# FFN up-projections of a two-layer hybrid decoder: one 512-column product for the rounded input and its residual

## The chip, the cores and the metric

The kernel runs on one core of one Trainium2 chip. The metric is the time of one execution on the device in microseconds (us). Three runs of the kernel before the change gave 2309.21, 2311.9 and 2316.67 us; the median is 2311.9.

PE below is TensorE (matrix products), DVE is VectorE, ACT is ScalarE, POOL is GpSimd, SP is SyncE, which issues the DMA transfers.

## The reference

Two decoder layers over a sequence of 256 tokens, width 2048. Each has a token mixer (layer 0: forgetting attention, layer 1: sliding-window attention with sinks) and then a gated feed-forward network (FFN) with a causal depthwise convolution of width 3. All is float32. The change touches the FFN:

```python
def conv_ffn(h, w_up, conv_w, conv_b, w_down):        # w_up (2048, 2*5632), w_down (5632, 2048)
    S = h.shape[1]
    u = h @ w_up
    up = jnp.pad(u, ((0, 0), (CONV_WIDTH - 1, 0), (0, 0)))
    u = sum(up[:, j:j + S] * conv_w[j] for j in range(CONV_WIDTH)) + conv_b
    g, val = u[..., :D_FF], u[..., D_FF:]
    return (jax.nn.silu(g) * val) @ w_down

for i in range(DEPTH):                                # DEPTH = 2
    mod = c_act @ ada_w[i] + ada_b[i]
    sh1, sc1, g1, sh2, sc2, g2 = jnp.split(mod[:, None, :], 6, axis=-1)
    h = x * (1.0 + sc1) + sh1
    y = fox_attention(h, ...) if i % N_MIXERS == 0 else swa_attention(h, ...)
    x = layer_norm(DEEPNORM_ALPHA * x + (1.0 + g1) * y, ln_mix_g[i], ln_mix_b[i])
    h = x * (1.0 + sc2) + sh2
    y = conv_ffn(h, ffn_w_up[i], ffn_conv_w[i], ffn_conv_b[i], ffn_w_down[i])
    x = layer_norm(DEEPNORM_ALPHA * x + (1.0 + g2) * y, ln_ffn_g[i], ln_ffn_b[i])
```

## The kernel before, in words

**Three products for one.** A float32 matrix is split into a rounded part (type fp32r, which PE takes in one pass) and the residual of the rounding, also fp32r. A product is then the sum of three: rounded × rounded, rounded × residual, residual × rounded. The FFN's input `h` lies transposed (features on the partitions) in `hH` (rounded) and `hL` (residual), two tiles of 16 chunks of 128 features by 256 tokens.

**The weight stream** (`stream`, L246 on). A weight tile is two chunks of 128 input features by 512 columns, 512 KB. For each tile SP issues one transfer into `w` (L256, ten buffers), ACT rounds it into `wh` (L259, four buffers), DVE subtracts to get the residual `wl` (L270, four buffers), and PE multiplies. The code lets casts and residuals of up to two tiles be written down ahead of the products of a tile (`ahead`, `settle`, `rest`).

**An up-projection** (`w_stationary`, `w_mm`) holds the weights in the array: `wh` or `wl` (128 × 128) is loaded and `hH` or `hL` (256 columns, the tokens) streams through. A block is 512 columns of the weights, that is four groups of 128 features, and takes eight tiles. Its four sums of 256 columns lie in two PSUM banks `ws`, two to a bank; a bank holds 512 float32 columns and there are eight. A tile has 2 chunks × 4 groups × 3 = 24 products. A layer has 22 such blocks, 11 for the gate and 11 for the value, in turn; both layers have 352 tiles.

**A down-projection** (`x_stationary`, `x_mm`) holds the activations and streams 512 columns of weights; a tile has 12 products, into banks `xs`.

**Evacuation** (`conv`, `evac`, `silu`, `gated` in `conv_ffn`). When a block is done, a generator is put in a list; each later tile steps every generator there once (`run_post`, called in `go`). For each group of 128 features, ACT computes the convolution's tap for the current token and the bias from PSUM into `u` (L987), and DVE adds the two earlier taps, reading PSUM again (L988, L990). One group is done every second tile. Gate blocks then take the SiLU (ACT, L1006, into `sil`); value blocks multiply by it (DVE, L1011) and split the result into the rounded and residual `gT` (L85 on ACT, L86 on DVE).

**Beside the FFN** the modulation vectors of later stages are computed: `ada_vector` streams `ada_w` (buffers `wa`, from the same pool as `w`) and DVE multiplies and adds (L385). In up-projections this goes at 0.52 steps per tile in layer 0 and 0.4 in layer 1, as long as there is work. A finished vector is summed over the partitions by PE into a bank `sm`; for a gate that is four products, each read by ACT (L397). In the first blocks of an FFN, DVE also does the layer norm's affine step on `x` (L604, L605), and PE transposes `x` into banks `sm` for `hH` and `hL`, two chunks at a time (L463).

**What sets the order.** The program is written with a tile framework: a scheduler puts each engine's instructions in a fixed order by priority and assigns buffers as they come free. On the chip each engine takes its list in that order and waits on semaphores.

Of the kernel before, what the change touches and what calls it, by code (L numbers as in the profile page):

```python
# [17 lines left out]
P = 128  # L18
# [23 lines left out]
def hybrid_trunk(ctx: ExitStack, tc: tile.TileContext, a: dict, out: bass.AP):  # L42
# [26 lines left out]
    def w_banks():  # L69
        return [bank("ws").rearrange("p (a s) -> p a s", a=2) for _ in range(2)]  # L70
# [180 lines left out]
    def stream(wsrc, row0, col, ks, use):  # L251

        for kc in ks[::2]:
            r0 = (row0 + kc) * P
            w = wtile()
            pin(nc.sync.dma_start(w, wsrc[r0:r0 + 2 * P, col:col + WB].rearrange("(k p) f -> p k f", p=P)), False)  # L256
            h = hl.tile([P, 2, WB], F32R, tag="wh", name="wh")
            l = hl.tile([P, 2, WB], F32R, tag="wl", name="wl")
            pin(nc.scalar.copy(h, w), False)  # L259

            def go(kc=kc, h=h, l=l):
                ahead[0] -= 1
                run_post()
                use(kc, h, l)
                if feeds:
                    feeds.pop(0)()
                tick()

            def residual_(w=w, h=h, l=l, go=go):
                pin(nc.vector.tensor_tensor(l, w, f32(h), op=ALU.subtract), False)  # L270
                del residuals[go]

            ahead[0] += 1
            weights.add(go)
            residuals[go] = residual_
            work.append(go)
            settle(2)
# [41 lines left out]

    def w_stationary(wsrc, col):  # L320

        ps = w_banks()
        stream(wsrc, 0, col, list(range(KC)), lambda kc, h, l: w_mm(ps, kc, h, l))
        return ps


# [122 lines left out]
            ada_step()  # L449


    hH = cst.tile([P, KC, S], F32R, name="hH")
    hL = cst.tile([P, KC, S], F32R, name="hL")
    cst.tile([P, 24], F32, name="gap")

    def mod_turn(k, n=1):
# [523 lines left out]
    def conv_ffn(l):  # L980
        w_up, w_dn = a["ffn_w_up"][l], a["ffn_w_down"][l]
        NB = DFF // WB
        cw = lambda j, f: ccol[:, l, j, f:f + 1]

        def conv(pf, f):
            u = tp.tile([P, S], F32, tag="u", bufs=3, name="u")
            nc.scalar.activation(u, pf, AF.Identity, bias=cw(CW, f), scale=cw(2, f))  # L987
            nc.vector.scalar_tensor_tensor(u[:, 1:], pf[:, :S - 1], cw(1, f), u[:, 1:],  # L988
                                           op0=ALU.mult, op1=ALU.add)
            nc.vector.scalar_tensor_tensor(u[:, 2:], pf[:, :S - 2], cw(0, f), u[:, 2:],  # L990
                                           op0=ALU.mult, op1=ALU.add)
            return u

        def evac(ps, f0, then):
            u = None
            for f in range(5):
                v = conv(ps[f // 2][:, f % 2, :], f0 + f) if f < 4 else None
                if u is not None:
                    then(f - 1, u)
                u = v  # L1000
                yield
                yield

        def silu(sil):
            def f_(f, u):
                nc.scalar.activation(sil[f // 2][:, (f % 2) * S:(f % 2 + 1) * S], u, AF.Silu)  # L1006
            return f_

        def gated(sil, gT):
            def f_(f, u):  # L1010
                nc.vector.tensor_tensor(u, u, sil[f // 2][:, (f % 2) * S:(f % 2 + 1) * S], op=ALU.mult)  # L1011
                g = gtile("gT")
                split(g[:, 0, :], g[:, 1, :], u)
                gT.append(g)
            return f_

        sbs = [(0, 6), (6, NB)]
        for si, (b0, b1) in enumerate(sbs):
            gT = []
            then(lambda: ada.update(rate=(0.52, 0.4)[l]))  # L1020
            for b in range(b0, b1):
                ps = w_stationary(w_up, b * WB)
                sil = [ttile("sil") for _ in range(2)]
                then(lambda ps=ps, b=b, sil=sil: defer(evac(ps, b * 4, silu(sil))))
                ps = w_stationary(w_up, DFF + b * WB)
                then(lambda ps=ps, b=b, sil=sil, gT=gT: defer(evac(ps, DFF // P + b * 4, gated(sil, gT))))

            def stat(kc, t, gT=gT):
                while kc >= len(gT):
                    run_post()  # L1030
                return gT[kc][:, 0, t * P:(t + 1) * P], gT[kc][:, 1, t * P:(t + 1) * P]

            def ready(si=si):
                if si == 0:
                    drain()
                ada_need(l, 5)
                ada["rate"] = (0.6, 0.4)[l]

            then(ready)
            for d in range(D // WB):  # L1040
                ps = x_stationary(w_dn, d * WB, b0 * 4, (b1 - b0) * 4, stat, (2, 4)[l] if si > 0 and d == D // WB - 1 else 0)
                then(lambda ps=ps, d=d, si=si: defer(residual(ps, d, gates[l, 5], si == len(sbs) - 1)))
        then(lambda: (flush(), ada.update(gate_free=True)))
# [54 lines left out]
```

## Time and profile before

| | |
|---|---|
| median of the runs | 2311.9 us |
| span of the profiled execution, from the first to the last instruction | 2317.4 us |
| instructions | 38661 |
| mean granted TensorE clock | 0.981 |
| DMA | 598.86 MB, 258 GB/s on average |
| layer 0: first up-projections, down-projection, second up-projections, down-projection | from 508, 786, 922 and 1152 us |
| layer 1: the same four | from 1558, 1837, 1968 and 2194 us |

The page gives no time of the profiled execution apart from its span. Up-projections run in two parts per layer, 6 gate and 6 value blocks and then 5 and 5, each followed by its share of the down-projection. In the views below, "busy" is the time in which an engine had an instruction running, "idle before" the time in which it waited ahead of a group of instructions, with what ended the wait. In rows of a chain or of a timeline, the first column is the start, the second the length, both in us.

### The profile page before, as it was taken

The page shows a single profiled execution, that of the slowest core. Times are in us where ns is not written, and L with a number is a line of the kernel's source. Part 1 is how long each engine was busy: PE and PEld are TensorE (multiplying, and loading weights), DVE is VectorE, ACT ScalarE, POOL GpSimd, SP SyncE. Part 2 cuts the span into 40 slices and gives each one's busy share as a digit, 9 for nine tenths or more (in the row PEclk, how much of TensorE's full clock was granted, in tenths as well). Part 3 has the DMA queues.
Part 4 walks back from the last instruction along what each step waited for, and adds up shares of the span by engine and source line. Part 5 has one row for each costly group of instructions (what it writes and reads, how often), then busy time and mean ns, then how long its engine had stood idle before and what let it go on. Part 6 is the DMA issues. An engine that isn't in the chain of part 4 may idle for free.

```text
span 2317.4 us, 38661 instructions
## 1 busy us (share of the span) xinstructions
PE 2243.1 (97%) x15061; PEld 2060.3 (89%) x15061; DVE 1804.0 (78%) x2609; ACT 1135.8 (49%) x1685; POOL 40.7 (2%) x79
## 2 busy tenths in 40 slices
PE   6899999999999999999999999999999999999997
PEld 5899998789999988999987778779999988999986
DVE  7788978879977876887887998899878655666655
ACT  1335654445555433454543478745555533454532
POOL 1001000010000000000001000000000000000000
PEclk9899999999999999999999999999999999999999
DMA  9998989968887897887897685778888566666663
GB/s 331 308 338 274 349 326 345 326 220 303 300 266 236 286 313 261 288 285 238 292 303 255 211 303 190 232 282 280 262 262 255 178 192 195 186 189 185 187 192 111
DMA packets 285561, 598.86 MB, mean 258 GB/s; under 512 B 20790, under 2 KB 53816, under 8 KB 285376
## 3 DMA queue, kind: packets, MB, share of 16 engines
q1 hardware_dynamic: 284768, 595.85, 78.1%
q8 instruction: 118, 1.93, 0.3%
q0 software_dynamic: 608, 0.53, 0.1%
q14 instruction: 67, 0.55, 0.1%
HBM read 594.21 MB, written 2.10 MB: 257 GB/s over the span
## 4 chain that ended last, share of the span: by engine, by line
PE 84%; DVE 10%; ACT 3%; issue 2%; DMA 1%; POOL 0%; SPq 0%; DVEq 0%; POOLq 0%; ACTq 0%
PE ws L76 49%; PE xs L76 30%; DVE wl L270 2%; DVE acc L385 2%; PE sm L76 1%; ACT wh L259 1%; PE cps L76 1%; PE o L76 1%; DVE oacc L518 1%; PE S L76 1%; PE sm L463 1%; ACT pr L645 0%; ACT pr L637 0%; PE T L657 0%; DVE x L563 0%
## 5 line engine op out<-in xcount | busy, mean ns | idle before, releaser
L270 DVE TENSOR_TENSOR wl<-w,wh 128x1024 fp32r<-128x1024 f32 x728 | 888.0, 1221 | 407.0 <-ACT wh L259 386.3
L259 ACT CAST wh<-w 128x1024 fp32r<-128x1024 f32 x728 | 762.9, 1051 | 864.6 <-PE ws L76 323.2
L76 PE MATMUL ws<-hH,wh 128*128 128x256 f32 x3328 | 945.8, 285 | 6.0 <-ACT wh L259 6.0
L76 PE MATMUL ws<-hH,wl 128*128 128x256 f32 x3328 | 936.9, 282 | 4.3 <-DVE wl L270 4.2
L76 PE MATMUL ws<-hL,wh 128*128 128x256 f32 x3328 | 939.5, 283 | 0.2 <-DVE hL L86 0.2
L76 PEld LDWEIGHTS ws<-hH,wh 128*128 128x128 f32 x3328 | 634.4, 191 | 10.0 <-ACT wh L259 6.8
L76 PEld LDWEIGHTS ws<-hH,wl 128*128 128x128 f32 x3328 | 637.2, 192 | 5.7 <-DVE wl L270 5.7
L76 PEld LDWEIGHTS ws<-hL,wh 128*128 128x128 f32 x3328 | 633.5, 190 | 2.7 <-issue 1.9
L76 PE MATMUL xs<-wh,gT 128*128 128x512 f32 x1408 | 437.2, 391 | 0.0
L385 DVE SCALAR_TENSOR_TENSOR acc<-wa,cact,acc 128x1024 f32<-128x1024 f32 x308 | 391.3, 1276 | 0.0
L76 PEld LDWEIGHTS xs<-wh,gT 128*128 128x128 f32 x1408 | 265.8, 189 | 55.4
L76 PE MATMUL xs<-wl,gT 128*128 128x512 f32 x704 | 275.1, 391 | 0.0
L76 PEld LDWEIGHTS xs<-wl,gT 128*128 128x128 f32 x704 | 133.0, 189 | 27.4
L76 PE MATMUL xs<-wl,hH 128*128 128x512 f32 x352 | 141.7, 403 | 5.5 <-DVE wl L270 5.5
L76 PE MATMUL xs<-wh,hL 128*128 128x512 f32 x352 | 140.8, 402 | 0.4 <-DVE hL L86 0.4
L76 PE MATMUL xs<-wh,hH 128*128 128x512 f32 x352 | 140.2, 408 | 0.2 <-ACT hH L473 0.2
L76 PE MATMUL xs<-wh,oT 128*128 128x512 f32 x384 | 125.4, 397 | 0.9 <-ACT pT L659 0.8
L987 ACT ACTIVATE u<-ws,ccol 128x256 f32<-128x256 f32 x176 | 96.5, 561 | 59.3 <-PE ws L76 52.0
L988 DVE SCALAR_TENSOR_TENSOR u<-ws,ccol,u 128x255 f32<-128x255 f32 x176 | 82.2, 476 | 20.5 <-ACT u L987 20.5
L76 PEld LDWEIGHTS xs<-wl,hH 128*128 128x128 f32 x352 | 67.8, 193 | 22.0 <-DVE wl L270 9.0
L76 PEld LDWEIGHTS xs<-wh,oT 128*128 128x128 f32 x384 | 72.8, 190 | 16.0 <-ACT pT L659 1.2
L990 DVE SCALAR_TENSOR_TENSOR u<-ws,ccol,u 128x254 f32<-128x254 f32 x176 | 83.1, 476 | 2.0
(211 smaller groups left out, 1564.4 us busy)
## 6 DMA issues: line engine op xcount, KB each, us to landing
w<-in_ffn_w_up_dram SPq DMA_DIRECT2D x352, 512.0 KB, 4.6
wa<-in_ada_w_dram SPq DMA_DIRECT2D x320, 512.0 KB, 5.1
w<-in_ffn_w_down_dram SPq DMA_DIRECT2D x176, 512.0 KB, 4.9
w<-in_fox_w_in_dram SPq DMA_DIRECT2D x96, 512.0 KB, 5.8
wo<-in_ada_w_dram SPq DMA_DIRECT2D x64, 512.0 KB, 6.5
w<-in_swa_w_in_dram SPq DMA_DIRECT2D x40, 512.0 KB, 4.9
w<-in_fox_w_o_dram SPq DMA_DIRECT2D x32, 512.0 KB, 6.3
w<-in_swa_w_o_dram SPq DMA_DIRECT2D x32, 512.0 KB, 5.5
```

What stands on the lines that cost most here:

```text
L76: return nc.tensor.matmul(o, lhsT, rhs, start=start, stop=stop, **kw)
L259: pin(nc.scalar.copy(h, w), False)
L270: pin(nc.vector.tensor_tensor(l, w, f32(h), op=ALU.subtract), False)
L385: pin(nc.vector.scalar_tensor_tensor(ac, wo, cact[:, k:k + 1], ac, op0=ALU.mult, op1=ALU.add), True)
L463: nc.tensor.transpose(o[:, t * P:(t + 1) * P], x[:, t, (k + j) * P:(k + j + 1) * P], ident)
L518: nc.vector.scalar_tensor_tensor(acc[:, v, k % 2, :], w[:, k, :], cact[:, kc:kc + 1], acc[:, v, k % 2, :], op0=ALU.mult, op1=ALU.add)
L987: nc.scalar.activation(u, pf, AF.Identity, bias=cw(CW, f), scale=cw(2, f))
L988: nc.vector.scalar_tensor_tensor(u[:, 1:], pf[:, :S - 1], cw(1, f), u[:, 1:], op0=ALU.mult, op1=ALU.add)
L990: nc.vector.scalar_tensor_tensor(u[:, 2:], pf[:, :S - 2], cw(0, f), u[:, 2:], op0=ALU.mult, op1=ALU.add)
```

## The change

`hH` and `hL` become the two halves of one tile `hHL`, so that for each chunk the rounded and the residual tokens lie side by side, 512 columns. One product of `wh` with these 512 columns takes the place of two of 256. Its sum is 512 columns wide and fills a bank: the left half collects rounded × rounded (and the residual weights' products), the right half rounded weights × residual tokens. A block thus takes four banks, named `wd`, instead of two. In a tile, the eight wide products come first, the eight with `wl` last. At the evacuation ACT copies the right half into a new tile `s`, and DVE adds the left half to it (`summed`); the convolution reads `s`. The generator's steps are placed anew: a group every tile, six steps in place of ten. The scratch for POOL's DMA descriptors goes to 1024. The first layer's attention keeps `w_banks` and `w_mm`.

```diff
--- before.py
+++ after.py
@@ -319,8 +319,17 @@
 
     def w_stationary(wsrc, col):
 
-        ps = w_banks()
-        stream(wsrc, 0, col, list(range(KC)), lambda kc, h, l: w_mm(ps, kc, h, l))
+        ps = [bank("wd") for _ in range(4)]
+
+        def use(kc, h, l):
+            cells = [(i, f) for i in range(2) for f in range(4)]
+            for i, f in cells:
+                mm(ps[f], h[:, i, f * P:(f + 1) * P], hHL[:, kc + i].rearrange("p a s -> p (a s)"),
+                   start=kc + i == 0)
+            for i, f in cells:
+                mm(ps[f][:, :S], l[:, i, f * P:(f + 1) * P], hH[:, kc + i, :], stop=kc + i == KC - 1)
+
+        stream(wsrc, 0, col, list(range(KC)), use)
         return ps
 
 
@@ -449,8 +458,8 @@
             ada_step()
 
 
-    hH = cst.tile([P, KC, S], F32R, name="hH")
-    hL = cst.tile([P, KC, S], F32R, name="hL")
+    hHL = cst.tile([P, KC, 2, S], F32R, name="hHL")
+    hH, hL = hHL[:, :, 0, :], hHL[:, :, 1, :]
     cst.tile([P, 24], F32, name="gap")
 
     def mod_turn(k, n=1):
@@ -982,23 +991,28 @@
         NB = DFF // WB
         cw = lambda j, f: ccol[:, l, j, f:f + 1]
 
-        def conv(pf, f):
+        def summed(pf):
+            s = tp.tile([P, S], F32, tag="s", bufs=3, name="s")
+            nc.scalar.copy(s, pf[:, S:])
+            nc.vector.tensor_tensor(s, pf[:, :S], s, op=ALU.add)
+            return s
+
+        def conv(s, f):
             u = tp.tile([P, S], F32, tag="u", bufs=3, name="u")
-            nc.scalar.activation(u, pf, AF.Identity, bias=cw(CW, f), scale=cw(2, f))
-            nc.vector.scalar_tensor_tensor(u[:, 1:], pf[:, :S - 1], cw(1, f), u[:, 1:],
+            nc.scalar.activation(u, s, AF.Identity, bias=cw(CW, f), scale=cw(2, f))
+            nc.vector.scalar_tensor_tensor(u[:, 1:], s[:, :S - 1], cw(1, f), u[:, 1:],
                                            op0=ALU.mult, op1=ALU.add)
-            nc.vector.scalar_tensor_tensor(u[:, 2:], pf[:, :S - 2], cw(0, f), u[:, 2:],
+            nc.vector.scalar_tensor_tensor(u[:, 2:], s[:, :S - 2], cw(0, f), u[:, 2:],
                                            op0=ALU.mult, op1=ALU.add)
             return u
 
         def evac(ps, f0, then):
-            u = None
-            for f in range(5):
-                v = conv(ps[f // 2][:, f % 2, :], f0 + f) if f < 4 else None
+            s = u = None
+            for f in range(6):
                 if u is not None:
-                    then(f - 1, u)
-                u = v
-                yield
+                    then(f - 2, u)
+                u = conv(s, f0 + f - 1) if s is not None else None
+                s = summed(ps[f]) if f < 4 else None
                 yield
 
         def silu(sil):
@@ -1083,7 +1097,7 @@
     from concourse import mybir as _mybir
     from concourse.bass_utils import run_bass_kernel_spmd as _run
 
-    nc = _bacc.Bacc("TRN2", target_bir_lowering=False, num_devices=1)
+    nc = _bacc.Bacc("TRN2", target_bir_lowering=False, num_devices=1, dynamic_dma_scratch_size=1024)
     arrays, args = {}, {}
     for name in _INS:
         v = _np.ascontiguousarray(inputs[name])
```

The scheduler's lists show what moved. The numbers behind names tell buffers apart; "waits" names the semaphores of an engine. First, PE's list at the start of the fourth block of layer 0's second part, before:

```order
L76 MATMUL ws_10300<-hH_125,wh_10304 128x256 [waits Activation_49]
L76 MATMUL ws_10300<-hL_126,wh_10304 128x256
L76 MATMUL ws_10300<-hH_125,wl_10305 128x256 [waits DVE_49]
L76 MATMUL ws_10300<-hH_125,wh_10304 128x256
L76 MATMUL ws_10300<-hL_126,wh_10304 128x256
L76 MATMUL ws_10300<-hH_125,wl_10305 128x256
L76 MATMUL ws_10301<-hH_125,wh_10304 128x256
```

and with the change:

```order
L76 MATMUL wd_9565<-hHL_125,wh_9571 128x512 [waits Activation_49]
L76 MATMUL wd_9566<-hHL_125,wh_9571 128x512 [waits PE_49]
L76 MATMUL wd_9567<-hHL_125,wh_9571 128x512 [waits PE_49]
L76 MATMUL wd_9568<-hHL_125,wh_9571 128x512 [waits PE_49]
L76 MATMUL wd_9565<-hHL_125,wh_9571 128x512
L76 MATMUL wd_9566<-hHL_125,wh_9571 128x512
L76 MATMUL wd_9567<-hHL_125,wh_9571 128x512
L76 MATMUL wd_9568<-hHL_125,wh_9571 128x512
L76 MATMUL wd_9565<-hHL_125,wl_9572 128x256 [waits DVE_49]
L76 MATMUL wd_9566<-hHL_125,wl_9572 128x256
```

The three narrow products of a group become a wide one at the head of the tile and a narrow one at its end; the first use of `wl` moves from the third product to the ninth.

Second, DVE's list in layer 0's first part, before the first residual (`wl_5652`) of the third block; `x` is the affine step, `acc` the modulation vector:

```order
L988 SCALAR_TENSOR_TENSOR u_5581<-ws_4977,ccol_120,u_5581 128x255
L270 TENSOR_TENSOR wl_5615<-w_5612,wh_5614 128x1024 [waits DMAHW5_49,PE_49,Activation_49]
L990 SCALAR_TENSOR_TENSOR u_5581<-ws_4977,ccol_120,u_5581 128x254 [waits DVE_49]
L604 SCALAR_TENSOR_TENSOR x_108<-x_108,ln_5354 128x512
L385 SCALAR_TENSOR_TENSOR acc_5129<-wa_5642,cact_111,acc_5129 128x1024 [waits DMAHW6_49]
L605 SCALAR_TENSOR_TENSOR x_108<-ln_5356,x_108 128x512 [waits DVE_49]
L604 SCALAR_TENSOR_TENSOR x_108<-x_108,ln_5354 128x512
L270 TENSOR_TENSOR wl_5652<-w_5649,wh_5651 128x1024 [waits DMAHW7_49,PE_49,Activation_49]
```

and with the change, where that residual is `wl_5563`, five rows further on:

```order
L1003 SCALAR_TENSOR_TENSOR u_5471<-s_5440,ccol_120,u_5471 128x255 [waits Activation_49]
L997 TENSOR_TENSOR s_5475<-wd_4978,s_5475 128x256
L1005 SCALAR_TENSOR_TENSOR u_5471<-s_5440,ccol_120,u_5471 128x254 [waits DVE_49]
L394 SCALAR_TENSOR_TENSOR acc_5122<-wa_5494,cact_111,acc_5122 128x1024 [waits DMAHW3_49]
L613 SCALAR_TENSOR_TENSOR x_108<-x_108,ln_5307 128x512
L270 TENSOR_TENSOR wl_5502<-w_5499,wh_5501 128x1024 [waits DMAHW4_49,PE_49]
L614 SCALAR_TENSOR_TENSOR x_108<-ln_5309,x_108 128x512 [waits DVE_49]
L1003 SCALAR_TENSOR_TENSOR u_5506<-s_5475,ccol_120,u_5506 128x255 [waits Activation_49]
L270 TENSOR_TENSOR wl_5531<-w_5528,wh_5530 128x1024 [waits DMAHW5_49,PE_49]
L1005 SCALAR_TENSOR_TENSOR u_5506<-s_5475,ccol_120,u_5506 128x254 [waits DVE_49]
```

Adds into `s` stand among the convolution's steps. From the start of the FFN's input up to that residual, there are four of them, and eight convolution steps where there were six; all other steps are as many as before.

Third, PE's list at the start of the ninth block of layer 0's first part, where the second of a gate's four sums comes between two blocks; before:

```order
L76 MATMUL ws_7054<-hH_125,wl_7306 128x256
L76 MATMUL sm_7404<-acc_5129,ones_84 128x512
L76 MATMUL ws_7336<-hH_125,wh_7340 128x256 [waits Activation_49]
L76 MATMUL ws_7336<-hL_126,wh_7340 128x256
L76 MATMUL ws_7336<-hH_125,wl_7341 128x256 [waits DVE_49]
```

and with the change:

```order
L76 MATMUL wd_6721<-hHL_125,wl_6922 128x256
L76 MATMUL sm_6994<-acc_5122,ones_84 128x512 [waits PE_49]
L76 MATMUL wd_6945<-hHL_125,wh_6951 128x512 [waits Activation_49]
L76 MATMUL wd_6946<-hHL_125,wh_6951 128x512 [waits PE_49]
L76 MATMUL wd_6947<-hHL_125,wh_6951 128x512 [waits Activation_49]
L76 MATMUL wd_6945<-hHL_125,wh_6951 128x512
L76 MATMUL wd_6948<-hHL_125,wh_6951 128x512 [waits Activation_49]
```

ACT's list at this place, with the change:

```order
L996 COPY s_7002<-wd_6718 128x256 [waits PE_49]
L996 COPY s_7031<-wd_6719 128x256 [waits PE_49]
L996 COPY s_7067<-wd_6720 128x256 [waits PE_49]
L406 ACTIVATE gate_6942<-sm_6994 128x512 [waits PE_49]
L1002 ACTIVATE u_7027<-s_7002,ccol_120 128x256 [waits DVE_49]
```

The bank of `sm_6994` is given to `wd_6948`, whose first product therefore waits for ACT's reading of the sum (L406); in ACT's list three copies stand ahead of it.

## The prediction

> **What bounds the kernel now.** I read the page first: busy time per engine, then which lines make up the chain that ended last.
>
> ```profile
> span 2317.4 us, 38661 instructions
> PE 2243.1 (97%) x15061; PEld 2060.3 (89%) x15061; DVE 1804.0 (78%) x2609; ACT 1135.8 (49%) x1685; POOL 40.7 (2%) x79
> PE ws L76 49%; PE xs L76 30%; DVE wl L270 2%; DVE acc L385 2%; PE sm L76 1%; ACT wh L259 1%; PE cps L76 1%; PE o L76 1%; DVE oacc L518 1%; PE S L76 1%; PE sm L463 1%; ACT pr L645 0%; ACT pr L637 0%; PE T L657 0%; DVE x L563 0%
> ```
>
> Half of the chain is matmuls into `ws`, the tiles that the change rewrites. A busy PE says little by itself, so next come the stretches: nearly all of both layers' up-projections.
>
> ```profile
> core 0: us, PE busy (x) PEld busy (x) DVE busy (x) ACT busy (x) POOL busy (x), PEclk, DMA share, GB/s
> 556.00:786.00 230.00, 229.64 (x1928) 227.52 (x1928) 188.67 (x243) 120.47 (x166) 0.00 (x0) 1.00 0.84 279
> 922.00:1151.00 229.00, 229.00 (x1949) 229.00 (x1948) 184.97 (x232) 114.83 (x153) 0.00 (x0) 0.99 0.83 275
> 1582.00:1837.00 255.00, 254.92 (x2142) 253.01 (x2143) 199.74 (x263) 133.80 (x184) 0.00 (x0) 1.00 0.78 253
> 1967.00:2194.00 227.00, 227.00 (x1925) 226.86 (x1924) 141.84 (x190) 114.84 (x154) 0.00 (x0) 1.00 0.64 187
> ```
>
> The reader is to see three things: PE has no gaps, its clock is full (1.00, 0.99), and no other engine is full (DVE 82% in the first row, ACT 52%, the DMA engines 84%). The chain in order of time then gives the pace of PE in long unbroken pieces:
>
> ```profile
> 1837.01 130.58 PE xs L76 x576
> 1967.59 226.13 PE ws L76 x1920
> 2193.72 103.37 PE xs L76 x456
> ```
>
> The 256-column products of an up-projection follow each other every 226.13 / 1920 = 117.8 ns; the 512-column ones of a down-projection every 103.37 / 456 = 226.7 ns (130.58 / 576 gives the same). Two narrow ones take 235.6, so a wide one in their place is 8.9 ns cheaper. That difference, multiplied, is the whole of the change's gain. The fixed share of 8.9 ns and 0.425 ns a column fit both paces.
>
> **The change part by part.**
>
> *Products.* Of a weight tile's 24 products of 256 columns, 16 become 8 of 512; 8 stay. Before: 24 × 117.8 = 2826.6 ns. After: 8 × 226.7 + 8 × 117.8 = 2755.7 ns. The difference, 70.9 ns, occurs in each of the 352 tiles: **25.0 us**. It lies on the path wherever PE has no gap, as in the four rows above. The wide product over `hHL` isn't in this trace. Its bounds are the down-projection's 226.7 ns (same shape, same types) and the 235.6 of the pair that it replaces, that is a gain of 25.0 or of nothing; I take 226.7, since only the names of the operands differ.
>
> A rule of the Trainium skill speaks for less. In "TensorE: Matmul & The Clock Gate", section "Wait — 56ns, not 53.3ns?", a warm matmul costs its columns plus a fixed 2.5 ns or so; a merged pair would save 2.5 ns, a tile 20 ns, all tiles 7.0 us, an estimate from that page. The rows above show 8.9 in this kernel, and they decide.
>
> *Evacuation.* Each group of 128 features (176 of them, four to a block) now needs a copy on ACT and an add on DVE ahead of the convolution, which then reads SBUF instead of PSUM. The nearest rows, two of them with a PSUM operand of this size:
>
> ```profile
> L85 ACT CAST oT<-o 128x256 fp32r<-128x256 f32 x12 | 4.4, 364 | 0.0
> L86 DVE TENSOR_TENSOR oT<-o,oT 128x256 fp32r<-128x256 f32 x12 | 5.0, 415 | 0.0
> L518 DVE SCALAR_TENSOR_TENSOR oacc<-wo,cact,oacc 128x256 f32<-128x256 f32 x192 | 79.9, 475 | 0.0
> ```
>
> So 0.36 us on ACT and 0.42 on DVE per group, half of that per tile (four groups to eight tiles). The convolution's DVE steps stay as long: 475 ns from SBUF here, 475 from PSUM below. Load in layer 0, the fullest: the first row of the stretches holds 1928 / 24 = 80.3 tiles, DVE 188.67 / 80.3 = 2.35 us per tile, with the adds 2.56; ACT 1.50, with the copies 1.68. PE will need 2.756. The cover therefore is thin on DVE (0.20 us per tile) and ample on ACT. What hides the adds are DVE's present idle times:
>
> ```profile
> L270 DVE TENSOR_TENSOR wl<-w,wh 128x1024 fp32r<-128x1024 f32 x83 | 101.2, 1219 | 35.9 <-ACT wh L259 33.7 <-DMA wa<-in_ada_w_dram 1.6
> L259 ACT CAST wh<-w 128x1024 fp32r<-128x1024 f32 x80 | 84.0, 1050 | 86.5 <-PE ws L76 79.4 <-issue 2.7 <-ACT u L987 2.4
> L990 DVE SCALAR_TENSOR_TENSOR u<-ws,ccol,u 128x254 f32<-128x254 f32 x41 | 19.5, 475 | 0.4
> L988 DVE SCALAR_TENSOR_TENSOR u<-ws,ccol,u 128x255 f32<-128x255 f32 x41 | 19.1, 475 | 4.1 <-ACT u L987 4.1
> ```
>
> DVE waits for the cast (33.7 us), the cast for PE to let go of a `wh` buffer (79.4): slack handed back, not a limit. The four `wh` buffers let casts and residuals run up to three tiles ahead, some 8 us, which carries the bursts of a block's evacuation. I cost the steady stretches at zero.
>
> *Order in a tile.* Residual weights are now wanted at the ninth product, 8 × 0.2267 = 1.81 us into a tile, where they were wanted at the third (0.24 us): 1.58 us more slack for DVE. This alone moves no time, as PE waits for `wl` hardly anywhere.
>
> *First blocks of layer 0.* There it does wait, and DVE has no gap ahead of it, because the layer norm's affine work (L604, L605) runs there too:
>
> ```profile
> PE ws L76 <- DVE wl L270: 0.4, 1, 0.4
> ```
>
> The first row is from the waits of PE between 500 and 600 us; the next are DVE's, in order of time.
>
> ```profile
> 552.03 0.47 DVE L990 SCALAR_TENSOR_TENSOR u<-ws,ccol,u 128x254 f32<-128x254 f32 x1
> 552.42 0.67 DVE L604 SCALAR_TENSOR_TENSOR x<-x,ln 128x512 f32<-128x512 f32 x1
> ...
> 555.42 1.21 DVE L270 TENSOR_TENSOR wl<-w,wh 128x1024 fp32r<-128x1024 f32 x1
> ```
>
> It is the third block's first residual. In the change's order (shown above) four adds and two more convolution steps stand ahead of it: 4 × 0.42 + 2 × 0.39 (552.03 to 552.42) = 2.46 us. PE arrives 16 × 0.0709 = 1.13 us earlier and can wait 1.58 longer. The wait becomes 0.4 + 2.46 + 1.13 − 1.58 = 2.4 us, **2.0 us more**. Bounds: 0, if DVE's queue has slack that the chain hides, and 5, if the next value block's adds find it still behind. In layer 1 PE did not wait for `wl` in its first blocks; I put nothing there.
>
> *Banks.* Two blocks of four now fill all eight, so any other PSUM tile comes between. The gate's four sums are such tiles:
>
> ```profile
> 686.74 0.86 PE sm L76 x2
> ```
>
> That is one sum in the chain; this is ACT's reading of it:
>
> ```profile
> L397 ACT ACTIVATE gate<-sm 128x512 f32<-128x512 f32 x16 | 9.4, 593 | 0.2 <-PE sm L76 0.2
> ```
>
> By that order the second gate sum's bank passes to the new block's fourth product. PE reaches it 0.86 + 4 × 0.23 = 1.8 us after the block before ended; ACT has three copies (3 × 0.36) and the gate (0.59) to do, 1.7 us. I put **0.5 us** for both layers, from nothing to 2. Elsewhere a block takes the banks of the block before last, evacuated a whole block's 22 us earlier.
>
> *DMA.* SP's queue keeps its order, and no transfer is added. The smaller scratch for POOL's descriptors concerns a few early loads, far from their use; nothing.
>
> Sum: −25.0 + 2.0 + 0.5 = **−22.5 us**. The profiled execution's span is 2317.4 us, 5.5 above the median of the runs (2311.9): 2294.9 in its terms, 2289.4 in the median's. I predict **2289.4 us**.
>
> **Rivals.**
>
> *DVE takes over in layer 0, in part.* Copy, add, `u`, convolution make two new hand-offs between ACT and DVE per feature group. The row of L988 shows 4.1 / 41 = 0.10 us waited per group at the one that exists. The limit is passed when DVE idles 0.40 us per feature group (0.20 per tile). At 0.50 a tile of layer 0 takes 2.81 us: 176 × 0.051 = 9.0 us back, 2298. For it: ACT and DVE take their work strictly in turn. Against it: other work stands between the hand-offs in the order.
>
> *The same, fully: slower.* Place: both steps of each hand-off in layer 0, and in layer 1's first half, where DVE has 199.74 / 89.3 + 0.21 = 2.45 us per tile. The gain is used up when the idle time passes 0.66 us per feature group (0.40 + 2 × 22.5 / 176). At 0.80, layer 0 needs 2.96 us a tile (+35.4) and layer 1's first 96 tiles 2.85 (+8.6): 2289.4 + 44 = 2333. Against it: 0.10 is measured today.
>
> *The fixed share is small.* Merging saves only what each product costs beside its columns. If a quarter of the 8.9 ns came off (a wide product over `hHL` at 233.4), 18 ns a tile or 6.3 us in all would remain, less the same 2.5 us of losses: 2308. Against it: two stretches of this trace agree on 226.7. The Trainium skill's page on TensorE, named above, would put the time there (20 ns a tile).
>
> *The change does nothing.* A wide product takes 235.6: only the losses remain, 2314. Nothing in the trace speaks for it.
>
> **How the numbers follow.** Forecast 0.72, DVE in part 0.13, small fixed share 0.05, nothing 0.04, slower 0.06. About 0.3% (6.9 us) is what a measurement can tell from no change; above 2318.8 is slower, below 2305.0 faster. Faster: 0.72 + 0.13 = 0.85; same: 0.09; slower: 0.06. The range begins at 2284 (the full 25 us, from the lowest run, 2309.2) and ends at 2302, which takes in DVE's partial limit and the losses' upper bounds (5 and 2).
>
> **What would show it.** Right: a piece of the second half of layer 1 with 8 wide and 8 narrow products in 2.756 us a tile, 220.5 us for its 80 tiles instead of 226.1; DVE near 2.56 us per tile in layer 0 with idle time left; a wait for `wl` of 2 to 3 us near 550. Wrong: wide products into `wd` at over 230 ns; PE idle on `wl` through layer 0's blocks; PE waiting for a bank at the start of many blocks rather than two.

## The result and the profile after

| | before | after |
|---|---|---|
| median of 11 runs each, us | 2310.5 (2301.2 to 2317.9) | 2300.3 (2297.6 to 2309.3) |
| span of the traced execution, us | 2317.4 | 2300.7 |

The ratio after to before is 0.9957, with a 95% interval of 0.9942 to 0.9972: about 10 us faster, where 22.5 were forecast. On another chip the same two kernels came to 2306.8 us (23 runs) and 2303.2 (10 runs, `a_again` below): a ratio of 0.9982, with an interval of 0.9965 to 0.9999, or 3.6 us. The gain is not one number, and the experiments show why. The time of a run is its span and some 1.8 us (2302.45 and 2300.7 for the traced execution of after), so the traced execution of before took about 2319.2 us, more than any of the eleven runs beside it. That will matter.

First the page of the changed kernel (span and busy time):

```profile
span 2300.7 us, 33462 instructions
PE 2225.8 (97%) x12245; PEld 1916.0 (83%) x12245; DVE 1852.9 (81%) x2785; ACT 1185.1 (52%) x1861; POOL 40.1 (2%) x79
```

PE is the bound as before, with 2816 products fewer. The same stretches as before the change, most of both layers' up-projections (columns as in the prediction):

```profile
556.00:786.00 230.00, 229.60 (x1311) 198.03 (x1310) 203.80 (x288) 134.35 (x210) 0.00 (x0) 1.00 0.86 284
922.00:1144.00 222.00, 222.00 (x1293) 193.77 (x1292) 191.19 (x264) 122.97 (x188) 0.00 (x0) 1.00 0.84 279
1582.00:1825.00 243.00, 243.00 (x1392) 210.23 (x1391) 206.15 (x299) 142.71 (x220) 0.00 (x0) 1.00 0.79 260
1967.00:2178.00 211.00, 211.00 (x1220) 183.88 (x1219) 144.63 (x216) 119.49 (x185) 0.00 (x0) 1.00 0.64 190
```

PE has no gaps but 0.4 us in the first row, its clock is full, and DVE has idle time left in each row. So nothing new holds PE up there: the time must be in PE's own pace. The chain in order of time gives it:

```profile
1572.37 210.89 PE wd L76 x1216
1825.55 130.57 PE xs L76 x576
1956.12 221.88 PE wd L76 x1280
2178.00 103.39 PE xs L76 x456
```

A tile of 16 products takes 221.88 / 80 = 2.7735 us. It took 2.8266 before, and 2.7557 was forecast. The down-projection keeps its 226.7 ns. PE's timeline shows which half of a tile is dear:

```profile
2050.26 2.02 PE L76 MATMUL wd<-hHL,wh 128*128 128x512 f32 x8
2052.13 1.07 PE L76 MATMUL wd<-hHL,wl 128*128 128x256 f32 x8
2053.04 2.02 PE L76 MATMUL wd<-hHL,wh 128*128 128x512 f32 x8
```

From start to start the eight wide products need 2052.13 - 2050.26 = 1.87 us, not 8 x 0.2267 = 1.81; the eight narrow ones 0.91, not 8 x 0.1178 = 0.94. Wide ones are slower than forecast, narrow ones faster. Taken product by product from the trace (time from one start to the next, ns; for after, medians by place in the tile, with the ninth product behind the bar; a tile's time on the right):

```
before, 1970-2190     24 x 117 to 119                                              2826.7
before, 1070-1144     24 x 113 or 114                                              2720.0
after,  1960-2170     226 236 231 236 231 236 231 236 | 118 113 113 113 113 113 113 113   2773.3
```

The second line is the discovery: the kernel before ran *the same products* at 113.3 ns in some stretches and at 117.8 in others, in one execution, at the same clock. The windows of its trace show it as well (columns as above):

```profile
922.00:1050.00 128.00, 128.00 (x1089) 128.00 (x1088) 106.16 (x129) 65.11 (x86) 0.00 (x0) 1.00 0.86 284
1070.00:1143.00 73.00, 73.00 (x647) 73.00 (x646) 63.20 (x85) 39.88 (x54) 0.00 (x0) 1.00 0.86 284
```

128.00 / 1089 is 117.5 ns, 73.00 / 647 is 112.8 (products cut by the window's edges count too). Below, the 113.3 ns of a narrow product and the 226.7 of a wide one are called undisturbed. 2 x 113.3 is 226.7: **an undisturbed wide product costs exactly two undisturbed narrow ones.** Between 256 and 512 columns there is no fixed share in a product that merging could save. What there is instead is extra time, which some products pay and others don't.

Against 2720.0, a tile of before at its slower pace, called late below, has 106.7 ns more and a tile of after 53.3. In before the 106.7 are spread evenly, some 4.45 ns on each of the 24 products. In after nearly all is in the wide products (232.7 ns on the average, the narrow ones 114.0). The change halves the extra time of a tile where the kernel before was late, and adds 53.3 ns where it was not.

### The profile page after: what moved, and what is told of

Same layout as the page of the kernel before. It is cut to its first block, busy times and chain, and to the rows that moved or that the text cites. A ratio compares the mean times of both kernels' runs of the same rounds, so it can differ in the third digit from the quotient of the medians.

```text
span 2300.7 us, 33462 instructions
## 1 busy us (share of the span) xinstructions
PE 2225.8 (97%) x12245; PEld 1916.0 (83%) x12245; DVE 1852.9 (81%) x2785; ACT 1185.1 (52%) x1861; POOL 40.1 (2%) x79
## 5 line engine op out<-in xcount | busy, mean ns | idle before, releaser
L76 PE MATMUL wd<-hHL,wh 128*128 128x512 f32 x2816 | 720.6, 398 | 3.0 <-DVE hHL L484 1.5
L76 PEld LDWEIGHTS wd<-hHL,wh 128*128 128x128 f32 x2816 | 505.6, 189 | 102.8 <-ACT hHL L482 3.7
L76 PEld LDWEIGHTS wd<-hHL,wl 128*128 128x128 f32 x2816 | 375.7, 189 | 33.0 <-DVE wl L270 0.8
L76 PE MATMUL wd<-hHL,wl 128*128 128x256 f32 x2816 | 380.3, 278 | 0.4 <-DVE wl L270 0.4
L76 PE MATMUL xs<-wh,hHL 128*128 128x512 f32 x704 | 235.3, 403 | 0.7 <-DVE hHL L86 0.4
L76 PE MATMUL ws<-hHL,wh 128*128 128x256 f32 x1024 | 194.2, 291 | 6.0 <-ACT wh L259 6.0
L76 PEld LDWEIGHTS ws<-hHL,wh 128*128 128x128 f32 x1024 | 163.8, 198 | 7.5 <-ACT wh L259 6.8
L76 PEld LDWEIGHTS xs<-wh,hHL 128*128 128x128 f32 x704 | 132.6, 190 | 28.9 <-DVE hHL L86 1.5
L76 PE MATMUL ws<-hHL,wl 128*128 128x256 f32 x512 | 145.9, 291 | 4.0 <-DVE wl L270 3.8
L76 PE MATMUL xs<-wl,hHL 128*128 128x512 f32 x352 | 141.6, 402 | 5.6 <-DVE wl L270 5.6
L1002 ACT ACTIVATE u<-s,ccol 128x256 f32<-128x256 f32 x176 | 104.2, 600 | 54.6 <-DVE s L997 53.3
```

The costliest lines, as they stand in the source:

```text
L76: return nc.tensor.matmul(o, lhsT, rhs, start=start, stop=stop, **kw)
L1002: nc.scalar.activation(u, s, AF.Identity, bias=cw(CW, f), scale=cw(2, f))
```

## The experiments

Theories. **Fixed share** (the prediction's): each product costs 8.9 ns beside its columns. **Order**: the extra time comes from changing bank and weights between wide products. **Place**: it depends on where PE's operands lie in a partition of SBUF; **collision** is its finer form, by the place of moving operand and weights against each other. **History**: at a given place PE has more than one pace and keeps one until something interrupts it.

All results ("tile" is the row of the chain for the second half of layer 1 divided by its 80 tiles; one run where no ratio stands):

| run | us | ratio to before, 95% | tile, us |
|---|---|---|---|
| a_again | 2303.2 | 0.9982 [0.9965, 0.9999] | 2.7735 |
| b_again | 2301.0 | | 2.8266 |
| a_split | 2305.5 | 0.9989 [0.9969, 1.0009] | 2.8266 |
| a_lead | 2314.6 | 1.0022 [1.0006, 1.0037] | 2.793 |
| b_lead | 2341.4 | 1.0147 [1.0125, 1.0170] | 2.880 |
| a_r0 | 2316.0 | 1.0034 [1.0015, 1.0054] | 2.793 |
| b_r0 | 2341.4 | 1.0162 [1.0133, 1.0191] | 2.880 |
| s_r0 | 2339.9 | 1.0150 [1.0123, 1.0178] | 2.880 |
| a_r64 | 2298.9 | | 2.757 |
| a_r32 | 2315.5 | | 2.807 |
| b_r32 | 2308.1 | | 2.800 |
| a_wl64 | 2321.3 | | 2.782 |
| b_hitch | 2289.1 | | 2.737 |
| b_hitch0 | **2288.1** | **0.9918 [0.9897, 0.9940]** | 2.736 |
| s_hitch | 2288.3 | 0.9923 [0.9896, 0.9949] | 2.736 |
| a_hitch | 2309.3 | 1.0004 [0.9988, 1.0019] | 2.784 |
| b_r0_hitch | 2345.5 | | 2.892 |
| b_h128 | 2285.2 | | 2.736 |

**Second traces.** Both kernels unchanged.

> The kernel before the change once more, for a second trace. Theory 'history': the stretches of 113.3 ns (531 to 556 us and 1068 to 1151 us in the first trace) lie elsewhere or have another length, and the time differs with them by 0.107 us a tile. Theory 'place' alone: the same stretches at the same paces. Theory 'fixed share': 117.8 ns throughout, which the first trace contradicts already.

> The changed kernel once more, on the same chip as the other three, for a second trace. Theory 'each tile restarts the pattern': the same 16 steps in every stretch, 2.7735 us a tile, within 0.01, though the kernel before changes its pace between executions; 2298 to 2309 us. Theory 'history' alone: other patterns in some stretches.

The kernel before, first trace, then second, from the chains of both:

```profile
556.68 130.06 PE ws L76 x1102
922.10 135.68 PE ws L76 x1152
1582.08 211.92 PE ws L76 x1797
1967.59 226.13 PE ws L76 x1920
```

```profile
553.64 125.17 PE ws L76 x1102
914.16 135.68 PE ws L76 x1152
1572.34 203.95 PE ws L76 x1797
1949.88 226.13 PE ws L76 x1920
```

The same 1797 products took 211.92 us in one execution and 203.95 in the other (117.9 and 113.5 ns each), the same 1102 took 130.06 and 125.17. The second and fourth row agree to 0.01 us: these pieces are entered straight from a down-projection, and are at 117.8 both times. So the pace is not drawn anew at each product: it is set at some event and kept, and at that event executions can differ. The two differing pieces make 13 of the 18 us between the two spans (2317.4 and 2299.2). Both begin behind a short wait of PE that the two executions share. At 556.68 and 553.64 it is one of 0.36 and 0.37 us for `wl`; in layer 1 it is this (first trace, then second):

```profile
1582.08 0.38 PE L76 MATMUL ws<-hL,wh 128*128 128x256 f32 x1 [0.19 <-DVE hL L86]
1572.34 0.39 PE L76 MATMUL ws<-hL,wh 128*128 128x256 f32 x1 [0.19 <-DVE hL L86]
```

Behind the same wait one execution went on at 117.8 and the other at 113.3. Why is not shown.

The changed kernel's pace is the same in all stretches of both its traces (221.88 us for the last 80 tiles in each). "History" holds for before; after, each tile restarts one pattern. Yet its two spans differ by 6.0 us (2300.7 and 2306.7), and its eleven runs by up to 12. Much of the 6.0 has another source, the granted clock (the column of 1.00 and 0.86; the trace of after first, then a_again):

```profile
1046.00:1070.00 24.00, 24.00 (x153) 21.41 (x152) 16.75 (x30) 12.40 (x19) 0.00 (x0) 1.00 0.66 204
1046.00:1070.00 24.00, 24.00 (x132) 21.32 (x131) 12.98 (x23) 10.13 (x16) 0.00 (x0) 0.86 0.57 183
```

0.14 of 24 us is 3.4 us; from 840 to 900 us the clocks are 1.00 and 0.97, another 1.8. So the pace is one source of the spread and the clock a second.

**Merging undone, all else kept.**

```
-                mm(ps[f], h[...], hHL[:, kc + i]..., start=kc + i == 0)
+                mm(ps[f][:, :S], h[...], hH[:, kc + i, :], start=kc + i == 0, ...)
+                mm(ps[f][:, S:], h[...], hL[:, kc + i, :], ...)
```

> The changed kernel with each wide product issued as two of 256 columns (hH into the first half of the bank, hL into the second): banks, evacuation, the late residual weights and all else as in the change, only the merging undone. Theory 'fixed share': 24 x 117.8 = 2.827 us a tile, 352 x 0.0535 = 19 us more than the changed kernel, about 2319 us. Theory 'place' and theory 'history' (PE has two paces of the same products, and keeps one until it is interrupted): no cost of a product as such, a tile anywhere between 24 x 113.3 = 2.719 us and 2.827, so 2281 to 2319 us, and stretches of pure 113.3 ns.

```profile
912.13 135.68 PE wd L76 x1152
1570.91 203.60 PE wd L76 x1794
1948.11 226.13 PE wd L76 x1920
```

Here too the second row has 113.5 ns a product and the others 117.8. "Fixed share" falls: it asked for 117.8 throughout and 2319 us. Merging alone comes to 2 to 5 us (2305.5 against 2303.2 and 2300.3, on different chips), which is less than the spread of either kernel's runs.

**The place of the operands.** One edit, ahead of hHL or hH, with other numbers each time; what follows keeps its place within 512 bytes (all weight tiles, gT and oT begin at multiples of 512; hH, hL and hHL of the two kernels stand 192 above one):

```
+    cst.tile([P, 16], F32, name="lead")
     hHL = cst.tile([P, KC, 2, S], F32R, name="hHL")
...
-    cst.tile([P, 24], F32, name="gap")
+    cst.tile([P, 8], F32, name="gap")
```

(16, 8): a_lead, b_lead. (80, 72): a_r0, b_r0, s_r0. (96, 56): a_r64. (88, 64): a_r32, b_r32.

> The changed kernel with hHL put 64 bytes further up, so that it begins at a multiple of 128 bytes of a partition, as the weight tiles and gT do (it began 64 bytes past one); the gap behind it is 64 bytes smaller, so nothing else moves. In the changed kernel's trace the wide products follow each other every 226, 236, 231, 236, 231, 236, 231, 236 ns and the narrow ones every 113.3, while the down-projection's wide ones (over gT) keep 226.7. Theory 'place' (the extra time depends on where PE's operands lie): all wide products at 226.7, a tile at 2.719 us instead of 2.7735, 352 x 0.0545 = 19 us less, about 2281 us. Theory 'fixed share' (the prediction's: each product has a fixed cost beside its columns) and theory 'order' (the extra time comes from the change of bank and weights from one wide product to the next): no change, a tile at 2.77 us and about 2300 us.

> The kernel before the change with hH and hL put 64 bytes further up, to multiples of 128 bytes, and the gap behind them 64 bytes smaller. Theory 'place': every product into ws at 113.3 ns instead of 117.8, a tile at 2.719 us instead of 2.827; the second half of layer 1 takes 217.6 us for its 80 tiles instead of 226.1; up to 352 x 0.107 = 37 us less, some 34 us since about 40 tiles ran at 113.3 already: about 2277 us, below the changed kernel. Theory 'fixed share': unchanged, 117.8 ns and about 2311 us. Theory 'history': both paces occur, about 2300 to 2318 us.

Place mattered, in the other direction than expected: 64 bytes further up the changed kernel was 11 us slower than a_again, and the kernel before 34 us slower, with every product of its up-projections at one pace, 120.0 ns, and its four runs within 4 us of each other (2340.4 to 2344.3). From the chain of b_lead:

```profile
1594.95 219.09 PE ws L76 x1824
1988.34 230.39 PE ws L76 x1920
```

> The changed kernel with hHL moved up by 320 bytes to a multiple of 512 bytes of a partition (everything behind it moves by 512 bytes, and so keeps its place within 512). Weight tiles, gT and oT all begin at multiples of 512; hHL stood at 192 above one in the changed kernel and at 256 in a_lead. Theory 'place, 0 is free': the down-projection's products over gT, at remainder 0, never leave 226.7 ns, so here wide products take 226.7 and narrow ones 113.3 all the time: a tile at 2.720 us, 352 x 0.0535 = 19 us below the changed kernel, 2281 to 2283 us. Theory 'place, equal remainders collide': slower than a_lead, over 2314 us, wide products above 233 on the average. Theory 'fixed share': 2300 us.

> The kernel before the change with hH and hL moved in the same way to multiples of 512 bytes. Theory 'place, 0 is free': 24 x 113.3 = 2.720 us a tile in every stretch, as much as 8 wide and 8 narrow products; about 2279 to 2283 us, and the spread of the runs shrinks, since there is one pace only. Then merging as such is worth nothing, and this kernel is within 3 us of a_r0. Theory 'equal remainders collide': 120 ns or more a product, 2341 us or more. Theory 'fixed share': 117.8 ns and about 2307 us, some 25 us above a_r0 if that has lost its extra time.

> a_split (merging undone, all else of the change kept) with hHL at a multiple of 512 bytes. Against a_r0 it shows what a merged product saves where neither pays extra time, against b_r0 what the change costs beside its products. Theory 'place, 0 is free': same time as a_r0 within 2 us, and 0 to 4 us above b_r0 (adds, copies, banks, first blocks). Theory 'fixed share': 352 x 0.071 = 25 us above a_r0.

> The changed kernel with hHL at 64 bytes above a multiple of 512. One more point of the map (so far 192: wide 232.7 on the average and narrow 114; 256: wide 230.1 and narrow 119). Theory 'place': a third pattern of the 16 steps of a tile, the same in every stretch, between 2.720 and 2.88 us. Theory 'order' (extra time from changing bank and weights alone): the changed kernel's pattern 226, 236, 231, 236 again.

The remainder 0 is not free; it gives what 256 above a multiple of 512 gave. The remainder 64 does not give what 192 gave. A period of 256 bytes fits these four points, one of 128 doesn't. Steps of a tile, as above:

```
a_lead, a_r0   233 236 228 233 231 227 227 227 | 113 119 120 120 120 120 120 120
b_lead, b_r0   24 x 120
a_r64          alternating tiles; wide 226 229 232 in turn, narrow 113.3 or 117.7
```

"Order" alone falls: the order is the same in after, a_r0 and a_r64, the pattern is not. The three kernels at remainder 0 have the cleanest comparison of the study, since each keeps one pace or one pattern. The chains of b_r0, then s_r0, then a_r0:

```profile
1990.56 230.39 PE ws L76 x1920
```

```profile
1985.64 230.39 PE wd L76 x1920
```

```profile
1965.67 223.44 PE wd L76 x1280
```

s_r0 differs from b_r0 in all that the change does except the merging: the same 230.39 us, and 2339.9 against 2341.4 us in all. Copies, adds, eight banks and late residual weights cost nothing that shows. a_r0 against s_r0 is the merging: 24 us less in all, because here each of 24 products pays 6.67 ns (2.880 us a tile, 160 ns above 2.720) and 73 ns of these are left after merging (2.793; 352 tiles at 87 ns less would be 30.5 us). At the kernel's own place the same edit saves 2 to 5.

> The changed kernel with hHL at 32 bytes above a multiple of 128. So far: 0 above one (a_lead, a_r0) 2.794 us a tile; 64 above one (the change, a_r64) 2.7735 and 2.758; without any extra time it would be 2.720. Theory 'collision' (the read of the moving operand and the load of the next weights get in each other's way, by the place of the one against the other): a pattern of its own between 2.72 and 2.80 us a tile; if halves of 128 bytes decide, it is like 0, 2.79 us and some 2315 us; if lines of 64 bytes matter, the moving operand now touches one more of them and the pattern moves at every product. Theory 'place does not matter below 64 bytes': the same as a_r0.

> The kernel before the change with hH and hL at 32 bytes above a multiple of 128. So far: at 0 every product into ws takes 120.0 ns in every stretch (2341 us), at 64 a stretch runs at 113.3 or at 117.8 (2301 to 2318 us). Theory 'collision': one pace or two between 113.3 and 120; if halves of 128 bytes decide, 120.0 again and 2341 us. Theory 'place does not matter below 64 bytes': the same as b_r0.

Halves of 128 bytes don't explain these: b_r32 would be at 120.0 ns and has 116.7, one pace in most pieces. a_r32 has the dearest tile of the merged kernels (2.807 us). Whether lines of 64 bytes play a part is not settled.

```
-            l = hl.tile([P, 2, WB], F32R, tag="wl", name="wl")
+            l = hl.tile([P, 2 * WB + 32], F32R, tag="wl", name="wl")[:, 16:16 + 2 * WB]
+            l = l.rearrange("p (k f) -> p k f", k=2)
```

> The changed kernel with hHL at a multiple of 512 as in a_r0 and the residual weights wl at 64 above a multiple of 128; the rounded weights wh stay at 0. In a_r0 the wide products come to 226.7 ns after five of them, the narrow ones run at 120. Theory 'collision by relative place': only the narrow products of the up-projections change, to 113.3 or 117.8, a tile falls from 2.794 us to 2.73 to 2.76; the products over wl in the down-projection, until now at 226.7, may rise to 229 to 232. Theory 'the place of hHL alone decides': pattern and pace of a_r0, 2.794 us.

```profile
1839.68 132.80 PE xs L76 x576
1972.48 222.53 PE wd L76 x1280
```

Against a_r0 only the residual weights moved (and, by multiples of 512, what lies behind them). A tile's narrow products, which load them, went from 119.1 to 117.9 ns on the average, the wide ones hardly changed (229.8 after 230.1), and the down-projection, undisturbed until now, rose from 226.7 to 132.80 / 576 = 230.6. The tiles now repeat in fours (2.803, 2.765, 2.780 and 2.779 us): a `wl` buffer has become 128 bytes longer, so that the weights of the four buffers begin at 64, 192, 320 and 448 above a multiple of 512. "The place of hHL alone" falls: the place of the weights counts too. That it is the one against the other fits all these runs, but none of them moves both together.

**An interruption.** One product of a block, over hL, in two pieces (in the mixers' blocks too):

```
+                if kc == 2 and i == f == 0:
+                    mm(o[:, :64], wh, hL[:, kc, :64], skip_group_check=True)
+                    mm(o[:, 64:], wh, hL[:, kc, 64:], skip_group_check=True)
+                else:
                     mm(o, wh, hL[:, kc + i, :], skip_group_check=True)
```

> The kernel before the change with one of its products of each block (of the second tile, over hL) issued as two pieces of 64 and 192 columns: a short interruption of the rhythm, nothing else. Theory 'history' (at this place PE has two paces, and an interruption settles which): stretches change their pace at this product, so that every block is at 113.3 or 117.8 from there on, in other stretches than in the two traces so far; all at 113.3 would be about 2281 us with 4 us for the interruptions, all at 117.8 about 2318. Theory 'the stage decides' (which engine or transfer is busy beside PE): the second half of layer 1 stays at 117.8, as in both traces, 226 us for its 80 tiles.

> The kernel before the change with the interruption in the first tile of a block instead of the second: one product over hL of each block issued as 64 and 192 columns. Theory 'history': the products run at 113.3 ns from the first tile of a block on, also behind the gate sums and at the start of the second halves, where b_hitch still ran some 60 tiles' worth of products at 117.8; 2285 to 2289 us, below both kernels of the change in every run. Theory 'chance' (b_hitch's one look was a lucky execution): times spread from 2289 to 2318 as the kernel's before.

In b_hitch the late pace came back with the gate's sums and with each entry from a down-projection, until the next block's interruption. In b_hitch0 `kc == 0` stands in the place of `kc == 2`. With it the pieces entered from a down-projection run at 113.3 too. Behind a gate sum inside a block the late pace still came back, against the expectation: 48 products in 5.66 us, 117.9 ns each, at 683.07 and at 696.02. From its chain:

```profile
915.30 131.34 PE ws L76 x1158
1570.28 205.20 PE ws L76 x1807
1949.12 218.88 PE ws L76 x1930
```

The last half of layer 1, 226.13 us in both traces of before, takes 218.88 with ten products more: 80 x 2.720 = 217.6, and 1.28 for the ten interruptions, 0.13 us each. (The expectation of b_h128 below has 28 ns for it. In the trace 28 ns is the whole step of the piece of 64 columns; the time is lost behind it, in steps of 170 and 141 ns.) All six runs (2285.5 to 2293.5) lie below all 23 of the kernel before beside them and below the lowest of after's. This beats both kernels of the change by undoing it and adding one product a block.

> The change's banks, evacuation and late residual weights, its wide products issued as two of 256, and the same interruption as b_hitch0, in the mixers too. Theory 'only the extra time of products matters': the same as b_hitch0 within 4 us (evacuation, banks and first blocks cost nothing to 2.5 us), so that the merged product, undone, saves 10 us or more against the changed kernel. Theory 'fixed share': at least 18 us slower than a_again.

2288.3 against 2288.1: with nearly all extra time gone, the change's evacuation and banks again cost nothing, and undoing its merging, with the interruption, saves 15 us (a_again on the same chip: 2303.2).

```
+                for c in ((0, 64), (64, 512)) if kc == 2 and i == f == 0 else ((0, 512),):
+                    mm(ps[f][:, c[0]:c[1]], h[...], r[:, c[0]:c[1]], start=kc + i == 0)
```

> The changed kernel with one wide product of each block (the first of the second tile) issued as 64 and 448 columns. Theory 'merged stretches have a pace without extra time too': the tiles behind it at 2.720 us, up to 19 us less, 2282 us. Theory 'each tile restarts the pattern' (the change from narrow to wide products is itself an interruption, once a tile, and the pattern that follows is always the same): 226, 236, 231, 236 again, 2.7735 us a tile, 2300 us.

```profile
1958.87 222.75 PE wd L76 x1290
```

The pattern 226, 236, 231, 236 came back in each tile behind the interruption; only the cost of ten of them was added (222.75 against 221.88). The merged stretch showed no undisturbed pace in any run.

> b_r0 (the kernel before, hH and hL at multiples of 512 bytes, 120.0 ns a product in every stretch) with the interruption of b_hitch0. Theory 'place sets the paces there are, an interruption picks one': 120.0 ns again, over 2335 us. Theory 'an interruption brings 113.3 at any place': about 2290 us.

> b_hitch0 with pieces of 128 and 128 columns instead of 64 and 192. Theory 'the short piece': in b_hitch0 the piece of 64 columns cost 28 ns more than its columns and the products behind it ran at 113.3; a piece of 128 columns that costs no such wait leaves the pace as it is, and stretches at 117.8 remain (2300 to 2318 us). Theory 'any break in the order': 113.3 from the first tile of a block on, about 2288 us.

b_r0_hitch: 120.0 ns again behind each interruption (1930 products in 231.39 us). So the interruption brings 113.3 only at a place that has this pace: the place limits which paces there are, and what ran ahead picks one of them. b_h128 does what b_hitch0 does, and its pieces of 128 columns cost as much (218.88 us for the same 1930 products). So the piece needn't be as short as 64 columns; whether one that costs nothing would do is not told by it.

## Why the prediction was right and wrong

**The step that failed** is the first: "Two narrow ones take 235.6, so a wide one in their place is 8.9 ns cheaper", with "The fixed share of 8.9 ns" behind it. 117.8 ns is not what a 256-column product costs. It is 113.3 and some 4.45 ns of extra time that the products paid in those stretches (twice this is the 8.9 ns). The wide product over hHL pays extra time as well: 232.7 ns on the average, not 226.7. Its narrow neighbours are down to 114.0. Instead of 70.9 ns a tile the change saves 53.3 where the kernel before is late. For all 352 tiles that would be 18.8 us instead of 25.0. That it pays extra time at all was within the bounds given for this product (226.7 to 235.6).

**The step that failed with it** is the carrying over from the traced execution to the median by a constant: "5.5 above the median". Nearly all tiles of the traced execution were at 117.8. The second one, with the two pieces at 113.5, took 2301.0 us. So much of the difference from the median was the very time that the change takes away, and where the kernel before runs at 113.3, the change loses 53.3 ns a tile. (The 5.5 also set a span against times of runs; with the 1.8 us between them it was 7.3.) Traced execution against traced execution the change gained 16.7 us, of which about 3 are due to the granted clock: it was 0.81 from 1050 to 1068 us in the trace of before and 1.00 from 1048 to 1068 in that of after. Before's execution was about 8.7 us above its median and after's 2.1 above, and 16.7 - 8.7 + 2.1 = 10.1 is the measured difference. The trace of before held the warning: 187 products in the 21 us from 534 to 555, and 89.54 us for 768 of them (116.6 ns each, although the clock is low at its start) in the chain at 1062. I took the three pieces that agreed.

That 2300.3 us lies within the range from 2284 to 2302 is luck. The upper part of the range was there for DVE's limit and for the waits for `wl` and for banks, and the missing gain went to none of these.

**Evacuation** at nothing: right, by s_r0 against b_r0 and s_hitch against b_hitch0. DVE came to 203.80 / (1311 / 16) = 2.49 us a tile in layer 0, forecast 2.56; the prices of copy and add were near:

```profile
L997 DVE TENSOR_TENSOR s<-wd,s 128x256 f32<-128x256 f32 x176 | 70.3, 418 | 0.0
L996 ACT COPY s<-wd 128x256 f32<-128x256 f32 x176 | 55.9, 371 | 1.0 <-DVE u L1005 1.0
```

**Order in a tile** without time: right. **First blocks**, 2.0 us more: wrong, the wait stayed at 0.4. In its place stands one that the prediction didn't see. PE's waits ahead of products into `wd` between 500 and 600 us:

```profile
PE wd L76 <- DVE hHL L484: 1.5, 1, 1.5
PE wd L76 <- DVE wl L270: 0.4, 1, 0.4
```

The first merged product of a layer needs hL too, where before it began with hH alone: 1.5 us, and 1.5 again in layer 1 (ACT hHL L482). So 2.0 was forecast for one place and 3.0 came at another. **Banks**, 0.5: nothing; between 680 and 712 us PE waited for no one.

**Rivals.** DVE took over nowhere. "The fixed share is small" was near for the wide product (233.4, measured 232.7), but it has 18 ns a tile, where 53.3 came off a late one, and its reason, a quarter of a fixed cost, is refuted. I gave it 0.05. On the rule weighed there: the Trainium skill ("TensorE: Matmul & The Clock Gate", section "Wait — 56ns, not 53.3ns?") gives a product its columns and a fixed 2.5 ns. The undisturbed paces here, 113.3 and 226.7 ns, are exactly one to two, so this kernel shows no fixed part beside the columns for these two widths.

**What stays open**: what inside PE the extra time is. That the read of the moving operand and the load of the next weights meet is argued from a_wl64 and the pace's dependence on both places, not shown. Why a gate sum or a down-projection was followed by 117.8 ns, a product in two pieces by 113.3, and a short wait by the one or the other is open too, and so is why the merged pattern has no undisturbed pace. One interruption a stretch instead of one a block was not tried.

## What to carry to other kernels

Before a pace is multiplied by a count, compare it over all long pieces of the trace and over two executions: where the same instruction has two durations at the same clock, the difference between them is not a property of the instruction, and a change that seems to remove it may only move it. In a stretch bound by PE, the place of its operands within 256 bytes (up to 160 ns of a tile's 2.72 us here) and an interruption of the rhythm are worth a try before the products are rewritten. A gain should be told against the kernel's distribution of runs, not against the one execution that was traced.

## What the runs showed of the hardware

Matmuls of the same shape took 113.3, 116.7, 117.8 or 120.0 ns from start to start, by no more than a shift of an operand by 32 or 64 bytes or by what ran ahead. Two of these paces can belong to one kernel: 13 of the 18 us between two executions of before. The granted clock is a second source of spread: some 5 of the 6 us between two executions of after. An additional product of 64 or 128 columns, at 0.13 us, held the undisturbed pace over whole blocks at one place (113.3 ns, b_hitch0 and b_h128), and not at another (120.0, b_r0_hitch).
